# A two-layer hybrid attention block: stick-breaking heads taken in pairs, side work given out by a budget, three products laid ahead in the second mixer

## The chip, the cores and the metric

The kernel runs on one core of a Trainium2 chip. The metric is the device time of one execution in microseconds. Before the change three runs gave 1328.83, 1330.05 and 1330.17 us.

## The reference, cut to what matters

Two layers work on `x` (512 tokens, width 1024, float32). Each layer is a mixer and a gated feed-forward, and both end in `x = layer_norm(ALPHA * x + (1 + g) * y)`. Shifts, scales and gates are six rows of 1024 a layer: `silu(c) @ w_mod + b_mod`.

The mixer of layer 0 ("even") projects `h` once and runs two kinds of attention side by side, eight heads of 64 columns each:

```python
# stick-breaking, a head h; past = key before query
z = q @ k.T / 8
log_keep = where(past, log_sigmoid(-z), 0)
suffix = reverse_cumsum(log_keep) - log_keep
w = where(past, exp(log_sigmoid(z) + suffix), 0)
o = w @ v
# indexed ("dsa"): a score of 4 index heads picks the 128 best keys of a query
score = sum_h relu(q_idx[h] @ k_idx.T / 8) * w_idx[h]
o = softmax(q @ k[top_k(score)].T / 8) @ v[top_k(score)]
```

The mixer of layer 1 ("odd") is differential attention: `softmax(q1 k1) - lam * softmax(q2 k2)`, then an RMS norm of each head. Both mixers end in a product with `w_out`. All is held to float32 accuracy: a large product is made as three products of rounded parts (high x high, low x high, high x low).

## The kernel before, in words

Tokens stand in four blocks of 128. TensorE (PE) makes all products; a weight is split by `split_w` (L291) into a high half by ScalarE (ACT) and a low half `wl = raw - wh` by an engine of the list `low`, which is VectorE (DVE) except in mixer 2. One step of a dense product (`dense`, L349) is three products of 512 columns; eight steps make one tile of 128 output columns. The next tile's split is asked for at the fourth step.

The program is written as generators. `weave(main, fill, ratio)` (L255) runs an attention generator and, for each cost that it yields, lets the fill generator issue as much dense work, by its own yielded costs. `beside(main, side, every)` (L271) gives a side generator a step on every so many steps. The numbers yielded are prices in us that the code assumes. The framework then plans each engine's own queue ahead of time: an instruction that is earlier in the program goes first, unless its inputs or its buffer are not there yet in the plan, in which case a later one that is ready may take its place. At run time each queue is strictly in order.

The parts that the change touches:

- `sb_heads` (L821) is the stick-breaking attention. A head's scores are held transposed in three PSUM banks (`za`, `zb`, `zc`), as four strips of keys (`STRIP`, L818: 512, 384, 256 and 128 columns of queries). `scores_of(h)` makes the four strips, each with a bias product, then by spans abs, exp, ln on ACT, a max-add on DVE, the rounded copy `hi` on DVE (L840) and `lo = l - hi` on GpSimd (POOL, L841). `suffix(h)` adds the sums of later keys by 20 products of `hi` and `lo` with constant matrices and takes exp to `w`. `mix(hp)` multiplies the weights of two heads with `v`. Even heads lie in rows 0 to 63 of `q` and `k`, odd heads in rows 64 to 127.
- `index_scores` and `top_keys` (L760, L784) make the index scores and pick keys in 48 steps on DVE. `mod_side` (L187) makes one row of shifts or gates: 16 products of DVE (`macc`, L211) and a reduction on PE. In layer 0 three such rows (`mods_even`, L996) run beside mixer 1; `topk` and they are handed out with `beside`, one `topk` step to each dense step, one mod step to every fourth and to each step of the heads.
- `dsa_heads` (L920) is the indexed attention, a pipeline of units of 128 queries and two heads. `one` makes scores, masks them, takes exp and normalises `e` on DVE (L952); `two`, two units later, transposes `e`; `three` multiplies with `v`. Its fill is `even_fill` (L1008): the rest of the projections, then the first half of the product with `w_out` (`down_beside`) with a mod step on every second step.
- `rope` (L454) turns a projected tile: ACT copies it to `rq`, DMAs on SyncE's queue swap halves into `rt`, DVE and POOL multiply, DVE adds.
- `down_last` (L613) ends a mixer: eight outputs of four terms each, of which `lead` outputs have three terms laid ahead (`down_lead`), behind the last transposes. `LEAD1` is 2 for mixer 1, `LEAD2` 5 for mixer 2. As a token block's two outputs are there, it is normed (DVE and POOL) and transposed for the next stage.
- `last_norm` (L1198) is the end of the kernel. For the last block two thirds are finished on DVE and 256 columns on POOL (L1212, L1213), each with its own transfer.

## Time and profile before

| | us |
|---|---|
| median of three runs | 1330.05 |
| profiled execution, its own time | 1333.3 |
| its span | 1331.5 |
| PE busy (share of the span) | 1285.6 (97%) |
| DVE busy | 877.8 (66%) |
| ACT busy | 498.0 (37%) |
| POOL busy | 250.7 (19%) |
| mean granted clock of PE | 0.985 |

The profile is one execution. Busy times of PE hold the time that a product is under way, so neighbours overlap; how long a run of products takes is read from the distance of their starts. The arrow behind an idle time names what ended it. One product in float32 makes two records of PE here, one in the rounded type makes one.

### The profile page before, as it was taken

The page shows a single profiled execution, that of the slowest core. Times are in us where ns is not written, and L with a number is a line of the kernel's source. Part 1 is how long each engine was busy: PE and PEld are TensorE (multiplying, and loading weights), DVE is VectorE, ACT ScalarE, POOL GpSimd, SP SyncE. Part 2 cuts the span into 40 slices and gives each one's busy share as a digit, 9 for nine tenths or more (in the row PEclk, how much of TensorE's full clock was granted, in tenths as well). Part 3 has the DMA queues.
Part 4 walks back from the last instruction along what each step waited for, and adds up shares of the span by engine and source line. Part 5 has one row for each costly group of instructions (what it writes and reads, how often), then busy time and mean ns, then how long its engine had stood idle before and what let it go on. Part 6 is the DMA issues. An engine that isn't in the chain of part 4 may idle for free.

```text
span 1331.5 us, 17598 instructions
## 1 busy us (share of the span) xinstructions
PE 1285.6 (97%) x6707; PEld 1020.7 (77%) x6707; DVE 877.8 (66%) x1596; ACT 498.0 (37%) x888; POOL 250.7 (19%) x177
## 2 busy tenths in 40 slices
PE   6999998999999999999999999898899999999997
PEld 4767676668888888888888866676798888888885
DVE  3789996988866665665694377688766435335357
ACT  2445554554532222222244355564543321222221
POOL 0113223001800000000017244442170000000034
PEclk9999989899999999999999999899899999999999
DMA  9952234333265555555423422215225222223221
GB/s 259 284 175 95 84 114 137 103 119 103 83 219 160 191 173 173 184 178 184 147 67 112 127 64 82 86 56 173 75 86 175 95 95 95 95 95 108 99 79 63
DMA packets 134532, 169.47 MB, mean 127 GB/s; under 512 B 7816, under 2 KB 89392, under 8 KB 134448
## 3 DMA queue, kind: packets, MB, share of 16 engines
q1 hardware_dynamic: 133712, 167.34, 39.2%
q8 instruction: 52, 0.85, 0.3%
q10 hardware_dynamic: 576, 0.98, 0.2%
q14 instruction: 32, 0.26, 0.1%
q0 software_dynamic: 160, 0.03, 0.0%
HBM read 159.95 MB, written 2.10 MB: 122 GB/s over the span
## 4 chain that ended last, share of the span: by engine, by line
PE 77%; DVE 11%; DMA 3%; ACT 3%; issue 2%; POOL 1%; SPq 1%; POOLq 0%; ACTq 0%; DVEq 0%
PE po L320 13%; PE po L321 13%; PE po L322 13%; PE pd L320 7%; PE pd L322 7%; PE pd L321 7%; PE pf L321 2%; PE pf L322 2%; PE pf L320 2%; DMA wm<-in_w_mod_dram 2%; PE pv L320 1%; PE pv L321 1%; PE pv L322 1%; DMA rt<-rq 1%; PE zq L893 1%
## 5 line engine op out<-in xcount | busy, mean ns | idle before, releaser
L294 ACT ACTIVATE wh<-raw 128x1024 fp32r<-128x1024 f32 x174 | 183.9, 1065 | 523.3 <-PE po L321 291.7
L320 PE MATMUL po<-hh,wh 128*128 128x512 f32 x848 | 340.9, 402 | 0.0
L321 PE MATMUL po<-hl,wh 128*128 128x512 f32 x848 | 333.4, 393 | 0.0
L322 PE MATMUL po<-hh,wl 128*128 128x512 f32 x848 | 333.4, 393 | 0.0
L298 DVE TENSOR_TENSOR wl<-raw,wh 128x1024 fp32r<-128x1024 f32 x169 | 228.5, 1356 | 157.1 <-ACT wh L294 156.6
L320 PEld LDWEIGHTS po<-hh,wh 128*128 128x128 f32 x848 | 160.8, 190 | 38.3 <-issue 6.4
L322 PEld LDWEIGHTS po<-hh,wl 128*128 128x128 f32 x848 | 161.0, 190 | 34.4
L321 PEld LDWEIGHTS po<-hl,wh 128*128 128x128 f32 x848 | 161.1, 190 | 30.4
L321 PE MATMUL pd<-wl,hid_h 128*128 128x512 f32 x352 | 137.1, 389 | 0.0
L322 PE MATMUL pd<-wh,hid_l 128*128 128x512 f32 x352 | 137.0, 389 | 0.0
L320 PE MATMUL pd<-wh,hid_h 128*128 128x512 f32 x352 | 137.0, 390 | 0.0
L211 DVE SCALAR_TENSOR_TENSOR macc<-wm,silu_c,macc 128x512 f32<-128x512 f32 x140 | 109.8, 787 | 7.0 <-DMA wm<-in_w_mod_dram 4.7
L636 DVE TENSOR_TENSOR sg<-sg,po 128x512 f32<-128x512 f32 x40 | 27.5, 687 | 125.3 <-PE po L322 125.3
L504 POOL TENSOR_TENSOR lnv<-lnv,mhalf 128x1 f32<-128x1 f32 x16 | 11.7, 731 | 396.8 <-DVE lnv L502 396.8
L320 PEld LDWEIGHTS pd<-wh,hid_h 128*128 128x128 f32 x352 | 66.1, 188 | 14.0 <-issue 0.4
L321 PEld LDWEIGHTS pd<-wl,hid_h 128*128 128x128 f32 x352 | 66.1, 188 | 13.7
L322 PEld LDWEIGHTS pd<-wh,hid_l 128*128 128x128 f32 x352 | 66.1, 188 | 13.6
L481 DVE TENSOR_TENSOR yt<-pd,grow 128x512 f32<-128x512 f32 x88 | 58.5, 681 | 10.7 <-PE pd L322 10.5
L600 POOL TENSOR_TENSOR raw<-raw,grow 128x1024 f32<-128x1024 f32 x4 | 10.4, 2610 | 284.0 <-DMA raw<-in_w_down_dram 283.6
L320 PE MATMUL pd<-wh,o_h 128*128 128x512 f32 x128 | 57.7, 451 | 1.8 <-DVE yt L481 1.8
L321 PE MATMUL pd<-wl,o_h 128*128 128x512 f32 x128 | 52.0, 406 | 0.3 <-DVE wl L298 0.3
L322 PE MATMUL pd<-wh,o_l 128*128 128x512 f32 x128 | 52.1, 407 | 0.0
(280 smaller groups left out, 2057.0 us busy)
## 6 DMA issues: line engine op xcount, KB each, us to landing
wm<-in_w_mod_dram SPq DMA_DIRECT2D x56, 512.0 KB, 4.9
raw<-in_w_gate_dram SPq DMA_DIRECT2D x22, 1024.0 KB, 5.2
raw<-in_w_up_dram SPq DMA_DIRECT2D x22, 1024.0 KB, 5.2
wm<-in_w_mod_dram SPq DMA_DIRECT2D x80, 256.0 KB, 4.0
raw<-in_w_down_dram SPq DMA_DIRECT2D x16, 1024.0 KB, 5.0
raw<-in_w_in_odd_dram SPq DMA_DIRECT2D x12, 1024.0 KB, 5.3
raw<-in_w_in_even_dram SPq DMA_DIRECT2D x6, 1024.0 KB, 7.6
raw<-in_w_down_dram SPq DMA_DIRECT2D x12, 512.0 KB, 3.3
```

Source lines behind the costliest of these rows:

```text
L211: dve.scalar_tensor_tensor(a, t[:, k, :], silu_c[:, k0 + k:k0 + k + 1], a, op0=OP.mult, op1=OP.add)
L294: act.activation(oh, src, AF.Copy)
L298: e.tensor_tensor(ol, src, oh, op=OP.subtract)
L320: pe.matmul(o, lhsT=ah, rhs=bh, start=start, stop=False, skip_group_check=True)
L321: pe.matmul(o, lhsT=ah, rhs=bl, start=False, stop=False, skip_group_check=True)
L322: pe.matmul(o, lhsT=al, rhs=bh, start=False, stop=stop, skip_group_check=True)
L481: dve.tensor_tensor(t, o, grow[:, cs], op=OP.mult)
L504: norm_done["pow"] = pool.tensor_tensor(y, v[:, 1:2], mhalf[:, 0:1], op=OP.pow).ins
L600: pool.tensor_tensor(tt, tt, gate[:, HALF[h]].unsqueeze(1).to_broadcast([P, 2, S]), op=OP.mult)
L636: dve.tensor_tensor(g, g, o, op=OP.mult)
L893: pe.matmul(z, lhsT=q[a][own, cs], rhs=k[b][own, :n], start=(g == 0), stop=(g == 2), skip_group_check=True)
```

## The change

1. The stick-breaking scores are made for both heads of a pair, strip by strip: all score products of a set of strips, then all bias products. The set is either banks `zb` and `zc` ("late") or `za` ("first"). The order of a pair is suffix late, suffix first, mix, then the next pair's late and first scores; the output's copy in `mix` thus stands ahead of the next late scores. `hi` is copied by ACT, one strip behind the strip that ACT works on (`cast`). The weights of the second head lie in other buffers (`weights_of`). The yielded prices are those of `SB_COST`.
2. `topk` and the mods of layer 0 are one generator, `sums`: a mod step after every three `topk` steps. `give(time)` advances it by a budget in us; the heads give at fixed places and `paced` gives 0.65 of each fill step. `beside` hands a mod step to every step of `down_beside`.
3. While the heads run, the low halves of weights are made by POOL (`low_on(pool)`).
4. In `dsa_heads` POOL normalises `e` in place of DVE.
5. In `rope` POOL writes its product to the target and DVE adds to it in place.
6. `LEAD2` is 3 in place of 5.
7. In `last_norm` DVE finishes the last 256 columns too.
8. `mod_side` yields once more ahead of each reduction in the narrow form; `top_keys` yields its price.

The diff, cut to its core; of the functions inside `sb_heads` the old lines are those printed above, so the new ones stand alone.

```diff
+SIDE = 0.65
+SB_COST = (6.2, 3.0, 2.8, 1.0)
...
-LEAD2 = 5
+LEAD2 = 3
@@ -210,8 +212,7 @@
                         else:
                             dve.scalar_tensor_tensor(a, t[:, k, :], silu_c[:, k0 + k:k0 + k + 1], a, op0=OP.mult, op1=OP.add)
                     yield
-            if wide:
-                yield
...
-            pool.tensor_tensor(q, q, cos_t, op=OP.mult)
-            dve.tensor_tensor(dst, q, t, op=OP.add)
+            pool.tensor_tensor(dst, q, cos_t, op=OP.mult)
+            dve.tensor_tensor(dst, dst, t, op=OP.add)
...
-                yield
+                yield 0.27 * (i + 1) + 0.28
...
@@ -819,64 +820,104 @@
     SPAN = ((0, 0, 512), (1, 512, 1024), (2, 1024, 1280))
     def sb_heads(qk):
+        Z, HL, W, todo = {}, {}, {}, []
+        def cast():
+            hi, lo, l = todo.pop(0)
+            act.activation(hi, l, AF.Copy)
+            pool.tensor_tensor(lo, l, hi, op=OP.subtract)
+        def scores_of(hp, banks):
+            q, k = qk[hp]
             need(q, k)
+            for i in banks:
+                for j in range(2):
+                    Z[hp, i, j] = bank("z" + "abc"[i])
+            strips = [(s, *STRIP[s]) for s in (1, 3, 2, 0) if STRIP[s][0] in banks]
+            for s, i, f, _, n in strips:
+                for j in range(2):
+                    own = slice(64 * j, 64 * j + 64)
+                    pe.matmul(Z[hp, i, j][:, f:f + n], lhsT=k[own, P * s:P * s + P], rhs=q[own, P * s:S],
+                              start=(f == 0), stop=False, skip_group_check=True)
+            for s, i, f, _, n in strips:
+                for j in range(2):
+                    pe.matmul(Z[hp, i, j][:, f:f + P], lhsT=ident_r, rhs=bias_sb_r, start=False, stop=True, skip_group_check=True)
+            for j in range(2):
+                if (hp, j) not in HL:
+                    HL[hp, j] = ab("hi", F32R), ab("lo", F32R)
+                hi, lo = HL[hp, j]
+                for i, a, b in SPAN:
+                    if i in banks:
+                        zi, e, l = Z[hp, i, j][:, :b - a], slice(a, b), wd("l")[:, :b - a]
+                        act.activation(l, zi, AF.Abs)
+                        act.activation(l, l, AF.Exp, scale=-1.0)
+                        act.activation(l, l, AF.Ln, bias=1.0)
+                        dve.scalar_tensor_tensor(l, zi, 0.0, l, op0=OP.max, op1=OP.add)
+                        todo.append((hi[:, e], lo[:, e], l))
+                        if len(todo) > 1:
+                            cast()
+            if todo:
+                cast()
+        def weights_of(hp, j, a, b):
+            part = a >= S
+            if (hp, j, part) not in W:
+                if j == 0:
+                    w = ab("w")
+                    W[hp, j, 0], W[hp, j, 1] = w[:, :S], w[:, S:]
+                elif part:
+                    W[hp, j, part] = T("row", [P, D], F32, 2, "w")
+                else:
+                    W[hp, j, part] = r1("w")
+            return W[hp, j, part][:, a - S * part:b - S * part]
+        def suffix(hp, banks):
+            for j in range(2):
+                hl = HL[hp, j]
+                for s in (0, 1, 3, 2):
+                    i, f, _, n = STRIP[s]
+                    if i not in banks:
+                        continue
+                    for s2 in range(s, 4):
+                        _, _, c2, n2 = STRIP[s2]
+                        for op in hl:
+                            pe.matmul(Z[hp, i, j][:, f + n - n2:f + n], lhsT=negtri_r if s2 == s else negones_r,
+                                      rhs=op[:, c2:c2 + n2], start=False, stop=True, skip_group_check=True)
+                for i, a, b in SPAN:
+                    if i in banks:
+                        act.activation(weights_of(hp, j, a, b), Z[hp, i, j][:, :b - a], AF.Exp)
         def mix(hp):
+            o = Z[hp, 0, 1]
             for s, (_, _, c0, n) in enumerate(STRIP):
                 for j in range(2):
                     h = 2 * hp + j
+                    pe.matmul(o[64 * j:64 * j + 64, S - n:S], lhsT=v_sb[s][:, 64 * h:64 * h + 64], rhs=weights_of(hp, j, c0, c0 + n),
                               start=(s == 0), stop=(s == 3), skip_group_check=True)
             put_o(hp, o)
+        late, first = (1, 2), (0,)
+        scores_of(0, late)
+        scores_of(0, first)
+        yield SB_COST[0]
         for hp in range(4):
+            suffix(hp, late)
+            give(1.7)
+            yield SB_COST[1]
+            suffix(hp, first)
+            give(1.7)
+            yield SB_COST[2]
+            mix(hp)
             if hp < 3:
+                give(1.8)
+                scores_of(hp + 1, late)
+                give(1.8)
+                yield SB_COST[3]
+                scores_of(hp + 1, first)
+                give(1.2)
+                yield SB_COST[0]
     turned = [None]
...
             for j in range(2):
-                dve.tensor_scalar(es[j], es[j], rr[:, j:j + 1], None, op0=OP.mult)
+                pool.tensor_scalar(es[j], es[j], rr[:, j:j + 1], None, op0=OP.mult)
...
     topk = late(2, chain(index_scores(), top_keys()))
     drain(beside(proj_tokens(W, 1024, evac_v), topk, 1))
-    rest = beside(even_rest(), topk, 1)
     got_rows = []
 
...
     mods0 = mods_even()
-    rest = beside(rest, mods0, 4)
-    weave(beside(sb_heads(qk_sb), mods0, 1), rest, SB_FILL)
+    def sums():
+        for n, cost in enumerate(topk):
+            yield cost or 1.5
+            if n % 3 == 2:
+                next(mods0, None)
+                yield 0.85
+        for _ in range(4):
+            next(mods0, None)
+            yield 0.85
+    owed, side = [0.0], sums()
+    def give(time):
+        owed[0] += time
+        while owed[0] > 0:
+            got = next(side, None)
+            if got is None:
+                break
+            owed[0] -= got
+    def paced(main, rate):
+        for cost in main:
+            give(cost * rate)
+            yield cost
+    rest = paced(even_rest(), SIDE)
+    low_on(pool)
+    weave(sb_heads(qk_sb), rest, SB_FILL)
+    low_on(dve)
     for _ in topk:
         pass
...
             next(mods0)
-        yield from beside(down_beside(w_out_even[0], 0, oT[:4], rows[0, 2], True), mods0, 2)
+        yield from beside(down_beside(w_out_even[0], 0, oT[:4], rows[0, 2], True), mods0, 1)
         drain(mods0)
...
-        for e, q, cs in (((dve, sp, slice(0, 384)), (dve, act, slice(384, 768)), (pool, sp, slice(768, D))) if b == 3
-                         else ((dve, sp, HALF[0]),)):
+        for q, cs in ((sp, slice(0, 384)), (act, slice(384, 768)), (sp, slice(768, D))) if b == 3 else ((sp, HALF[0]),):
             t = xa[b][:, cs]
-            if e is dve:
-                dve.scalar_tensor_tensor(t, t, r, rows["b"][:, cs], op0=OP.mult, op1=OP.add)
-            else:
-                pool.tensor_scalar(t, t, r, None, op0=OP.mult)
-                pool.tensor_tensor(t, t, rows["b"][:, cs], op=OP.add)
+            dve.scalar_tensor_tensor(t, t, r, rows["b"][:, cs], op0=OP.mult, op1=OP.add)
             away(q, b, cs)
```

## Rows read from the trace of the kernel before

**Rows 1.** The page, part 1: busy us (share of the span) and instructions.

```profile
PE 1285.6 (97%) x6707; PEld 1020.7 (77%) x6707; DVE 877.8 (66%) x1596; ACT 498.0 (37%) x888; POOL 250.7 (19%) x177
```

**Rows 2.** Stretches of two stages: us, busy time of each engine, clock, DMA share.

```profile
95.90:228.70 132.80, 131.10 (x589) 90.83 (x588) 116.37 (x249) 71.29 (x138) 35.80 (x30) 0.95 0.35 110
228.70:301.90 73.20, 68.31 (x468) 46.82 (x468) 63.67 (x177) 38.62 (x100) 7.17 (x6) 0.95 0.34 112
```

**Rows 3.** PE in order of time, one head's scores: start us, us, what, count.

```profile
105.45 1.12 PE L830 MATMUL za<-q_sb,k_sb 64*128 64x512 f32 x2
106.51 0.33 PE L832 MATMUL za<-cst_r 128*128 128x128 f32 x1
106.76 0.91 PE L830 MATMUL zb<-q_sb,k_sb 64*128 64x384 f32 x2
...
109.33 0.44 PE L320 MATMUL po<-hh,wh 128*128 128x512 f32 x1
```

**Rows 4.** PE in order of time, two index heads one behind the other.

```profile
92.11 0.92 PE L777 MATMUL ix<-kix,qix 64*128 64x384 f32 x4
```

**Rows 5.** Stretches of lower granted clock (the column behind the busy times).

```profile
144.70:148.10 3.40, 3.40 (x9) 2.61 (x8) 3.40 (x9) 2.23 (x6) 0.66 (x1) 0.51 0.03 11
233.50:240.30 6.80, 6.59 (x30) 3.77 (x30) 5.33 (x18) 2.21 (x9) 0.59 (x1) 0.50 0.36 105
```

**Rows 6.** What PE waited for, whole span: us in total, times, longest.

```profile
PE zq L893 <- DVE kd_l L929: 4.3, 1, 4.3
PE po L1144 <- DVE on L1134: 4.0, 3, 2.6
```

**Rows 7.** Groups by line, 96 to 228 us: busy us, mean ns, idle before.

```profile
L841 POOL TENSOR_TENSOR lo<-l,hi 128x512 fp32r<-128x512 f32 (+1 forms) x24 | 27.5, 1151 | 84.4 <-DVE hi L840 58.2 <-PE ix L777 22.1 <-issue 4.1
L837 ACT ACTIVATE l<-l 128x512 f32<-128x512 f32 (+1 forms) x24 | 12.6, 560 | 0.3
L298 DVE TENSOR_TENSOR wl<-raw,wh 128x1024 fp32r<-128x1024 f32 x10 | 12.1, 1208 | 0.0
L294 ACT ACTIVATE wh<-raw 128x1024 fp32r<-128x1024 f32 x10 | 10.6, 1061 | 10.8 <-PE po L321 10.6
L840 DVE CAST hi<-l 128x512 fp32r<-128x512 f32 (+1 forms) x24 | 9.5, 407 | 0.0
L810 ACT ACTIVATE o_h<-ot 128x512 fp32r<-128x512 f32 x4 | 2.5, 632 | 0.1
```

**Rows 8.** Groups by line on POOL, whole span.

```profile
L298 POOL TENSOR_TENSOR wl<-raw,wh 128x1024 fp32r<-128x1024 f32 x5 | 12.4, 2480 | 7.0 <-ACT wh L294 3.7 <-issue 3.3
```

**Rows 9.** PE in order of time, end of mixer 2.

```profile
946.12 0.39 PE L321 MATMUL pd<-wl,o_h 128*128 128x512 f32 x1
946.34 0.39 PE L322 MATMUL pd<-wh,o_l 128*128 128x512 f32 x1
948.41 0.63 PE L523 MATMUL tx<-ct,xa 128*128 128x128 f32 x4 [1.69 <-DVE xa L509]
950.71 0.80 PE L320 MATMUL pd<-wh,o_h 128*128 128x512 f32 x1 [1.67 <-DVE yt L481]
```

**Rows 10.** Groups by line on DVE in the indexed stage.

```profile
L211 DVE SCALAR_TENSOR_TENSOR macc<-wm,silu_c,macc 128x512 f32<-128x512 f32 x9 | 6.9, 761 | 0.4 <-DMA wm<-in_w_mod_dram 0.4
```

**Rows 11.** One line's instructions: duration ns min/median/max, first and last start.

```profile
L952 DVE TENSOR_SCALAR e<-e,rr x32: 278/406/1411, 238.9 to 293.0; 128x128 f32<-128x128 f32 x8, 128x256 f32<-128x256 f32 x8, 128x384 f32<-128x384 f32 x8, 128x512 f32<-128x512 f32 x8
```

**Rows 12.** DVE in order of time, the last block.

```profile
1325.89 1.14 DVE L1210 SCALAR_TENSOR_TENSOR xa<-xa,lnv,lnb 128x384 f32<-128x384 f32 x2
```

**Rows 13.** POOL in order of time, the last block.

```profile
1326.15 1.60 POOL L1212 TENSOR_SCALAR xa<-xa,lnv 128x256 f32<-128x256 f32 x1 [0.43 <-DVE xa L1205]
1327.83 0.72 POOL L1213 TENSOR_TENSOR xa<-xa,lnb 128x256 f32<-128x256 f32 x1
```

**Rows 14.** DVE in order of time, beside POOL work.

```profile
991.88 3.41 DVE L298 TENSOR_TENSOR wl<-raw,wh 128x1024 fp32r<-128x1024 f32 x1
```

**Rows 15.** POOL in order of time, the same stretch.

```profile
991.36 6.19 POOL L543 TENSOR_TENSOR xa<-xa,lnb 128x1024 f32<-128x1024 f32 x2
```

46 lines of the change are left out of this document (1 added, 45 removed).

## The prediction

> **What bounds the kernel now.** I read the page's busy shares first, then the stretches, then single stretches of TensorE in order of time. TensorE (PE) is busy for 1285.6 of 1331.5 us [rows 1], so only two things can shorten the kernel: less time of PE per product, or less waiting in the few places where PE stands. The edits of any weight lie in two stages [rows 2]: stick-breaking attention from 95.9 to 228.7 us (132.8 us; PE 131.1 busy, DVE 116.4, ACT 71.3, POOL 35.8) and the indexed attention behind it (73.2 us; PE 68.3, DVE 63.7, POOL 7.2). So PE sets the pace of both, with DVE close behind it. The profiled execution took 1333.3 us, 1.8 outside the span and 3.25 above the median of 1330.05; I sum differences and take them from the median.
>
> **Scores by pairs (the main term).** In the old order one head's scores run alone: four products of 64 rows, each followed by a bias product of 128 rows, from 105.45 to the next fill product at 109.33, so 3.88 us a head and 7.76 a pair [rows 3]. A lone head's 384-column strip keeps PE 0.91 us (2 records). In the index scores, two heads that stand in different row halves are issued one behind the other: their two 384-column products take 0.92 us together (4 records) [rows 4]. So two row halves work at once, and the second head of a strip is nearly free. The new code issues the two heads of a strip one behind the other. For a pair I count: the 1280 columns of one head, 3.0 us in proportion to the 0.91 us of 384 columns, less the changes of shape that fall away as strips follow each other: I take 2.4; eight bias products in two runs of one shape, at under half of the 0.25 us that each keeps PE alone, from start to next start [rows 3]: 0.9 with their changes. That is 3.3 us, 4.45 less than 7.76, and 17.8 for four pairs. Bounds: if nothing overlapped, only changes of shape would go (some 0.6 us a head by the bias rows, 4.8 in all); if bias and changes cost nothing, 5.3 a pair, 21.
>
> **Clock.** In four stretches of 3.4 us of this stage the granted clock is about 0.5 (1.2 of 2.4 GHz), one is shown, and so it is in one of 6.8 us behind the wait at its end [rows 5]. Each 3.4 us at the lower level costs 1.7. The first of the four, at 100, follows a lone head's scores; the one at 233.5 follows PE's 4.3 us stand for kd_l [rows 6]. Paired scores leave fewer half-used stretches: I take two of four away, -3.4 us; bounds -10.2 (all, the seam's too) and +3.4 (two more).
>
> **New waits in the stage.** DVE loses the 24 casts (9.5 us) and the ten low halves of weights (12.1) and is no longer near its bound; ACT gains the 24 casts, about 24 x 0.56 = 13.4 us (0.63 each by the copy o_h, 0.56 with the narrow strips), and POOL ten subtractions of 2.48, 24.8 us [rows 7, 8]. ACT then has 85 and POOL 61 us of a stage of some 112: neither is a bound by its sum. As a chain it is tight: from late scores to their low halves ACT makes 4 strips x 3 passes x 0.56 + 4 casts x 0.56 = 9.0 us, then POOL 1.15 [rows 7], so about 10; PE has one fill step, the first strip's scores (1.2 by the same count) and ten steps between, at 0.68 a step (three products some 0.23 apart [rows 9]) 8.7 us. The second head's part is needed 1.4 us later, which about closes it. I take +1 us a pair, +4. Below, 0. Above, one weight split ahead of the strip on ACT (1.06) and one on POOL (2.48) at each of eight suffix calls: 28. Copying outputs ahead of the late scores only changes which of ACT's work comes first, and frees the bank that the first strip needs; 0.
>
> **Side sums.** The give() budget is 3.4 + 4.8 us a pair and 0.65 of each fill step; counting the yields, 44 of 49 top-key steps and 14 of 54 mod steps are out by the end of the weave, so five selection steps (0.82 us each by the code's own price, an order of size) and 26 more products of macc (0.76 [rows 10]) come into the indexed stage or into DVE's new slack ahead of it. No instruction is added, only order: the extra yield, SIDE and the changed beside() likewise. Against it stand the 32 normalisations that leave DVE (median 0.41 [rows 11], 13 us). DVE's 63.7 us of 73.2 become 63.7 - 13 + 20 + 4 = 75 if nothing is done ahead. But the stage before has over 30 us of DVE to spare, so I expect most to be done there. POOL needs for a 128x256 normalisation between 0.72 (its two-input neighbour) and 1.60 (the same operation, beside DVE work) [rows 12, 13]; in proportion to the columns (10,240 in all) 29 to 64 us for all 32. I take the lower end: the larger row runs beside a DVE operation for half of its time. A unit's transposes come two units later, some 9 us, which hides 2 x 1.3 of the widest; only the last unit shows. +1 us; bounds -4.3 (PE's stand for kd_l at the seam goes [rows 6]) and +29 (below). At the seam itself DVE stood for the landing of a rope transfer, which stays; 0.
>
> **Rope.** POOL writes its product to the target rather than in place; same instructions, one buffer free earlier. 0, bounds -1 and +1.
>
> **Three products laid ahead in mixer 2.** 18 products (4.1 us) move from before the last head's output to behind it. Before, PE ran out of work twice while the first blocks were normed: 1.69 us for xa L509 and 1.67 for yt L481, starts 948.41 and 950.71 [rows 9]. The first block can close up to 4.1 us sooner with 18 products still to come, so both stands (3.4 us) should be covered: -3.4. What is lost is cover ahead of the last head's output, where PE already stands 2.6 us for `on` [rows 6]; before that stand only some 19 of the 45 products were issued (counted in order of time), and 27 still suffice. Bounds -5.1 (a clock stretch with them) and +4.1 (all 18 missed).
>
> **The last quarter.** POOL's two operations end at 1328.55; DVE's second piece ends at 1327.03 and a third of 256 columns adds about 0.4 (two of 384 take 1.14) [rows 12, 13]: 1327.4, -1.1 us. Bounds -1.5 and 0 (if the transfer of the second piece ends last).
>
> **Sum.** -17.8 - 3.4 + 4 + 1 - 3.4 - 1.1 = -20.7; 1330.05 - 20.7 = 1309 us.
>
> **Rivals.**
> *The chain behind the scores takes half back.* If in each pair one split sits ahead of the strips on ACT and POOL (3.5 us), +14 in place of +4, and after each such stand a clock stretch (1.7) in place of the two removed: 1309 + 10 + 3.4 + 1.7 = 1324. For it: ACT's 9 us against PE's 8.7. Against: the order is planned, and PE waited hardly at all in this stage.
> *More goes than I count.* All four clock stretches and the seam's wait and stretch go too: 1309 - 3.4 - 4.3 - 3.4 = 1298. For it: DVE is freed. Against: the seam hung on a transfer.
> *POOL takes DVE's time (slower).* A DVE subtraction of 128x1024 that takes 1.21 as a rule [rows 7] took 3.41 beside POOL [rows 14, 15]. In the indexed stage 35 macc, five splits and eight xa sums of DVE have two inputs in SBUF; beside POOL the split loses 2.2, the others, half as wide, 1.1: 5 x 2.2 + 43 x 1.1 = 58 us if all are hit in full. At 1.60 us for 256 columns POOL is busy 64 us of 73; nearly each is hit then, but on average half way through, so 29 us fall on a DVE that is already full: 1309 - 1 + 29 = 1337. It is slower than before from about 22 us on: a POOL busy two thirds of the stage, with DVE's side work still in it. Against it: DVE's slack one stage ahead. The Trainium skill ("SBUF — State Buffer", two separate sides) states that rule: DVE operations with two SBUF inputs and GpSimd operations share one port pair, whoever starts first holds it for the whole instruction. The two rows of the split agree with it. Against it speaks the Trainium skill in "GPSIMD Engine Reference", engine selection: one-input work on GpSimd runs at about line rate, by which, as an estimate, a 256-column normalisation is near 0.2 us and the 32 take under 10; the row of 1.60 speaks against the page, and no row shows the operation undisturbed.
> *The pairs don't overlap.* The four-pass products come apart in the planned order or don't run at once: only the changes of shape are saved, 4.8 of 17.8, so 1322. The index rows speak against it.
>
> **Numbers.** Forecast (1301 to 1317) 0.60, half taken back 0.18, more 0.11, slower 0.07, no overlap 0.04. The range 1295 to 1324 leaves out the slower case and the far ends. A measurement of this kernel tells 0.2%, some 2.7 us, from no change: the first, the third and the last case are faster, of the second 0.14 (the rest of it 0.03 same and 0.01 slower): faster 0.89, same 0.03, slower 0.08.
>
> **What would show it.** Pair scores near 3.3 us with the two heads' starts some 10 ns apart; the stage near 113 us; hi on ACT, wl on POOL at about 2.5; no stand of PE at 948 to 951; the last transfer 1 us earlier. I am wrong if PE shows stands for `lo` or `wl` of several us in each pair, if the indexed stage grows beyond 80 us with DVE full, or if `e` on POOL holds the transposes.

## The result and the profile after

The changed kernel took 1339.65 us (median of 4 runs, 1336.95 to 1341.31), the kernel before 1329.65 beside it: a ratio of 1.0055 with a 95% interval of 1.0031 to 1.0079. It is slower by some 7 us by the ratio, where 21 less were forecast.

The page's first part, to set beside [rows 1]: TensorE is busy 16.7 us less, and the span (1339.4) is 7.9 longer. So its work went down, and waiting came in its place.

```profile
PE 1268.9 (95%) x6707; PEld 1011.1 (75%) x6707; DVE 867.0 (65%) x1531; ACT 506.3 (38%) x912; POOL 319.9 (24%) x217
```

The two stages of [rows 2], cut at the same places (0.5 us ahead of the first score, the first indexed score, 3.8 us behind the last indexed output). The columns are as there: length, busy time of each engine, clock, DMA share.

```profile
95.70:234.30 138.60, 116.23 (x579) 85.53 (x578) 100.12 (x203) 80.05 (x161) 56.24 (x39) 0.90 0.29 87
234.30:318.30 84.00, 75.84 (x505) 52.02 (x505) 63.24 (x163) 39.71 (x105) 43.21 (x35) 0.92 0.45 143
```

TensorE works 15 us less in the first stage, which is 5.8 longer; no other engine is full by its sum. The second is 10.8 longer with VectorE's work as before. In marks: from first score to last mix 125.6 us against 129.1, from there to the first indexed score (the seam) 12.4 against 3.1, indexed scores and outputs 80.2 against 69.4. Behind them the kernel gains: 3.8 in the differential stage, 5.3 at the end of mixer 2, 0.9 at the end.

One pair's scores in TensorE's order of time, to set beside one head's in [rows 3] (start, us, what, count of records):

```profile
96.22 1.03 PE L841 MATMUL zb<-q_sb,k_sb 64*128 64x384 f32 x8
97.09 0.60 PE L841 MATMUL zc<-q_sb,k_sb 64*128 64x256 f32 x4
97.62 0.66 PE L845 MATMUL zb<-cst_r 128*128 128x128 f32 x4
98.12 0.39 PE L845 MATMUL zc<-cst_r 128*128 128x128 f32 x2
98.43 1.13 PE L841 MATMUL za<-q_sb,k_sb 64*128 64x512 f32 x4
99.49 0.44 PE L845 MATMUL za<-cst_r 128*128 128x128 f32 x2
99.77 0.45 PE L321 MATMUL po<-hh,wh 128*128 128x512 f32 x1
```

A pair takes 3.55 us (96.22 to 99.77), against 7.76. The pairs overlap as forecast.

What TensorE waited for from 96 to 345 us, where [rows 6] has one wait of 4.3 in the same part of the kernel (in total, times, longest). `macc` is a modulation sum, `mh` and `ml` are its high and low half, which TensorE adds up; `hi` and `lo` are the halves of the stick-breaking sums:

```profile
PE pm L223 <- DVE ml L221: 6.5, 1, 6.5
PE pm L231 <- DVE macc L213: 3.8, 1, 3.8
PE ix L778 <- ACT w L890: 3.7, 1, 3.7
PE zb L886 <- POOL lo L829: 3.5, 6, 1.0
PE po L321 <- ACT q_sb L471: 3.4, 1, 3.4
PE pm L222 <- ACT mh L220: 2.9, 2, 2.4
```

And the waits behind these, of VectorE, of ScalarE (96 to 225) and of SyncE's load queue:

```profile
DVE macc L213 <- DMA wm<-in_w_mod_dram: 22.5, 15, 4.6
```

```profile
ACT hi L828 <- DVE l L856: 16.8, 8, 5.1
```

```profile
SPq L559 <- POOL wl L299: 44.5, 2, 28.4
```

The 2.4 us for `mh` and the 6.5 us for `ml`, at the seam, are not a wait for a sum: the last product of this sum began at 140.5. ScalarE made `mh` only at 224.80. VectorE made `ml` at 232.39, behind two products of the next sum that waited for their loads, a split and a mask step (ScalarE, then VectorE):

```profile
224.80 0.62 ACT L220 ACTIVATE mh<-macc 128x512 fp32r<-128x512 f32 x1
```

```profile
225.73 1.82 DVE L213 SCALAR_TENSOR_TENSOR macc<-wm,silu_c,macc 128x512 f32<-128x512 f32 x1 [1.40 <-DMA wm<-in_w_mod_dram]
230.39 0.75 DVE L213 SCALAR_TENSOR_TENSOR macc<-wm,silu_c,macc 128x512 f32<-128x512 f32 x1 [2.84 <-DMA wm<-in_w_mod_dram]
...
232.39 0.69 DVE L221 TENSOR_TENSOR ml<-macc,mh 128x512 fp32r<-128x512 f32 x1
```

The clock falls beside the stands. Two stretches, to set beside [rows 5]; the column behind the busy times is the granted clock, 0.50 is 1.2 GHz. The first begins 0.8 us behind three short stands (0.77, 0.91 and 0.31 us, for `hi` and `lo`), and the 3.7 us for `ix` lie in it. The second begins 1.1 us behind a stand of 2.4 us for `mh`, and the 6.5 us for `ml` lie in it:

```profile
110.60:124.30 13.70, 8.70 (x27) 6.47 (x27) 13.46 (x25) 8.06 (x16) 7.61 (x5) 0.50 0.43 131
226.60:243.70 17.10, 9.76 (x36) 5.94 (x36) 11.85 (x33) 5.81 (x18) 5.18 (x6) 0.50 0.46 154
```

Between the first score and the first feed-forward 44.4 us run at half clock, against 20.5 before.

The end of mixer 2: of the two stands in [rows 9] (1.69 and 1.67 us) one of 0.48 is left. And the last block on VectorE: its three pieces end at 1336.24, 4.7 us behind TensorE's last product; before, GpSimd ended 5.8 behind it [rows 13].

```profile
961.46 1.53 PE L524 MATMUL tx<-ct,xa 128*128 128x128 f32 x12 [0.48 <-DVE xa L510]
```

```profile
1334.71 1.53 DVE L1277 SCALAR_TENSOR_TENSOR xa<-xa,lnv,lnb 128x384 f32<-128x384 f32 x3
```

### The profile page after: what moved, and what is told of

Read it like the earlier page. It is cut to its first block, busy times and chain, and to the rows that moved or that the text cites. A ratio compares the mean times of both kernels' runs of the same rounds, so it can differ in the third digit from the quotient of the medians.

```text
span 1339.4 us, 17581 instructions
## 1 busy us (share of the span) xinstructions
PE 1268.9 (95%) x6707; PEld 1011.1 (75%) x6707; DVE 867.0 (65%) x1531; ACT 506.3 (38%) x912; POOL 319.9 (24%) x217
## 4 chain that ended last, share of the span: by engine, by line
PE 66%; DVE 15%; DMA 7%; ACT 5%; issue 4%; SPq 2%; POOL 1%; DVEq 0%; ACTq 0%; POOLq 0%
PE po L321 12%; PE po L322 12%; PE po L323 12%; PE pd L321 7%; PE pd L322 7%; PE pd L323 7%; DMA wm<-in_w_mod_dram 4%; DVE score L792 2%; DVE wl L299 2%; DVE macc L213 2%; DVE top L791 1%; DMA rt<-rq 1%; PE pv L321 1%; PE pv L322 1%; PE pv L323 1%
## 5 line engine op out<-in xcount | busy, mean ns | idle before, releaser
L299 DVE TENSOR_TENSOR wl<-raw,wh 128x1024 fp32r<-128x1024 f32 x159 | 224.6, 1416 | 173.9 <-ACT wh L295 173.6
L323 PEld LDWEIGHTS pd<-wh,hid_l 128*128 128x128 f32 x352 | 66.1, 188 | 13.7
L322 PEld LDWEIGHTS pd<-wl,hid_h 128*128 128x128 f32 x352 | 66.1, 188 | 13.7
```

The costliest lines, as they stand in the source:

```text
L299: e.tensor_tensor(ol, src, oh, op=OP.subtract)
L322: pe.matmul(o, lhsT=ah, rhs=bl, start=False, stop=False, skip_group_check=True)
L323: pe.matmul(o, lhsT=al, rhs=bh, start=False, stop=stop, skip_group_check=True)
```

## The experiments

Four edits, alone and together, put a part of the changed kernel back. They are named C, S, L and E here. Theories have letters of their own in the expectations, and the text always says "theory" with those:

```diff
# C: the cast on VectorE
-            act.activation(hi, l, AF.Copy)
+            dve.tensor_copy(hi, l)
# S: the side sums handed out as before
-    rest = paced(even_rest(), SIDE)
+    rest = beside(beside(even_rest(), topk, 1), mods0, 3)
-    weave(sb_heads(qk_sb), rest, SB_FILL)
+    weave(beside(sb_heads(qk_sb), mods0, 1), rest, SB_FILL)
-    owed, side = [0.0], sums()
+    owed, side = [0.0], iter(())
# L: the low halves of weights on VectorE
-    low_on(pool)
-    low_on(dve)
# E: the normalisation on VectorE
-                pool.tensor_scalar(es[j], es[j], rr[:, j:j + 1], None, op0=OP.mult)
+                dve.tensor_scalar(es[j], es[j], rr[:, j:j + 1], None, op0=OP.mult)
```

S is near the old order, not the same: the kernel before has a modulation step at every fourth fill step and more steps of the heads. By the last mix 38 of the 48 modulation products had run before, 21 in the changed kernel, 41 with S and 38 in the plain kernel.

**All runs in one table.** The stage is the time from the first score to the last mix; "stands" is TensorE's idle time in it, "half" its time at half clock, both added up over the profiled execution. "Own" is the stage less the stands and less half of the time at half clock: roughly what TensorE's products would take at full clock (roughly, since some stands lie in half-clock time). "Next" runs from the last mix to the last indexed output. The kernel before was timed beside each, and ratios are to be compared rather than medians; single profiles of one kernel differ by some us, so that a few us of one column alone prove nothing. Each edit also lets all queues be planned anew, so part of a small difference can be the new plan and not the part that was edited.

| kernel | us | ratio (95%) | stage | stands | half | own | next |
|---|---|---|---|---|---|---|---|
| before | 1329.65 | | 129.1 | 1.7 | 13.7 | 120.5 | 72.5 |
| changed | 1339.65 | 1.0055 (1.0031 to 1.0079) | 125.6 | 13.5 | 20.5 | 101.9 | 92.6 |
| C | 1342.1 | 1.0108 (1.0085 to 1.0131) | 128.2 | 16.1 | 23.9 | 100.2 | 92.3 |
| S | 1334.15 | 1.0032 (1.0009 to 1.0055) | 141.9 | 22.7 | 37.5 | 100.5 | 70.4 |
| L | 1337.35 | 1.0066 (1.0045 to 1.0087) | 124.7 | 13.5 | 20.5 | 101.0 | 91.8 |
| C S L | 1327.78 | 0.9985 (0.9967 to 1.0002) | 127.9 | 11.2 | 23.9 | 104.8 | 76.5 |
| C S L E, "plain" | 1321.62 | 0.9937 (0.9914 to 0.9960) | 127.9 | 12.7 | 20.5 | 105.0 | 70.7 |
| C S | 1334.19 | 1.0031 (1.0014 to 1.0047) | 136.8 | 18.3 | 30.7 | 103.2 | 73.6 |
| S L | 1327.73 | 0.9991 (0.9977 to 1.0004) | 133.8 | 18.4 | 27.3 | 101.8 | 71.8 |
| before, tail parts alone | 1325.66 | 0.9973 (0.9953 to 0.9993) | 127.0 | 0.1 | 13.7 | 120.1 | 73.6 |
| plain, one ScalarE pass | 1320.14 | 0.9927 (0.9897 to 0.9958) | 126.3 | 11.6 | 20.5 | 104.5 | 67.1 |
| before, one ScalarE pass | 1325.93 | 0.9983 (0.9954 to 1.0011) | 126.3 | 1.5 | 10.2 | 119.7 | 68.5 |
| C L E (sums new) | 1334.31 | 1.0026 (1.0005 to 1.0047) | 124.0 | 14.3 | 17.1 | 101.2 | 86.5 |
| plain, fill moved | 1326.36 | 0.9969 (0.9945 to 0.9993) | 129.6 | 13.6 | 20.5 | 105.8 | 72.8 |
| plain, half the keys | 1325.51 | 0.9959 (0.9936 to 0.9982) | 133.0 | 15.2 | 27.3 | 104.2 | 70.9 |
| before, half the keys | 1332.71 | 1.0005 (0.9979 to 1.0031) | 131.7 | 0.3 | 27.3 | 117.8 | 71.4 |
| S L E (cast on ScalarE) | 1322.66 | 0.9950 (0.9928 to 0.9973) | 135.8 | 18.6 | 27.3 | 103.6 | 65.6 |
| plain, mod steps later | 1327.69 | 0.9985 (0.9968 to 1.0002) | 127.8 | 15.3 | 20.5 | 102.3 | 71.8 |
| plain, max-adds first | 1326.29 | 0.9981 (0.9960 to 1.0003) | 135.1 | 16.3 | 27.3 | 105.2 | 67.2 |
| plain, both reliefs | 1314.71 | 0.9879 (0.9837 to 0.9921) | 123.9 | 11.8 | 17.1 | 103.6 | 66.9 |

**C: the cast on VectorE.**

> One line of the changed kernel is put back: the 24 casts hi run on VectorE behind their max-add, not on ScalarE. Theory A (ScalarE's queue stands for VectorE): in the changed kernel hi on ACT waits 16.8 us in 8 places for the max-add l, the longest 5.1, and TensorE stands behind it for ix (3.7) and q_sb (3.4), with half-clock stretches of 13.7 and 6.8 us after them. Then the waits of hi, ix and q_sb go, and the stick-breaking stage is shorter by 7.1 plus about half of 20.5 of clock, some 10 to 17 us: about 1325. Theory B (side sums come late): the cost lies at the seam and in the indexed stage, which this leaves as they are: the stage of the pairs gains at most 3, the time is 1336 to 1340, and zq still starts more than 9 us after the last mix.

It is slower: 1.0108, 7 us by the ratios, with intervals that lie apart. Theory A falls. Its row was right as a row, its reading was not: the cast stood 5.11 us because its input, the max-add, was late on VectorE, and on either engine it stands behind that. The stretch shows it (ScalarE, then VectorE, then GpSimd of the changed kernel):

```profile
99.79 0.94 ACT L855 ACTIVATE l<-l 128x512 f32<-128x512 f32 x2
...
106.88 0.63 ACT L828 ACTIVATE hi<-l 128x512 fp32r<-128x512 f32 x1 [5.11 <-DVE l L856]
```

```profile
98.70 2.20 DVE L213 SCALAR_TENSOR_TENSOR macc<-wm,silu_c,macc 128x512 f32<-128x512 f32 x1
...
106.17 0.67 DVE L856 SCALAR_TENSOR_TENSOR l<-zb,l 128x512 f32<-128x512 f32 x1
```

```profile
97.82 2.53 POOL L299 TENSOR_TENSOR wl<-raw,wh 128x1024 fp32r<-128x1024 f32 x1 [6.14 <-ACT wh L295]
```

ScalarE's last pass over this strip ends by 100.7; its max-add L856 begins at 106.17, behind index sums, top-key steps and modulation products of VectorE.

**S: the side sums as before.**

> The changed kernel, with only the handing out of the side sums as before: one top-key step at each fill step, one step of the modulation sums at each step of the heads and at every third fill step (42 of the 54 by count before the weave ends, against 14); no give(). Theory B: the macc products are spread over the stage of the pairs, their loads are done when the seam comes, so pm no longer stands for mh, ml and macc (2.4 + 6.5 + 3.8 us at 225 to 233 and 311), and the 17.1 us at half clock behind it go too: seam -9, indexed stage -8 to -11, time 1320 to 1324. Theory A: ScalarE's queue is the cause; the seam gains 3 at most, time 1334 to 1340, hi still waits some 16 us for l.

The seam and the indexed stage came back as theory B said (70.4 us against 92.6), but the stage of the pairs took 141.9: with the 18 modulation products that return to it (35 against 17) it is 16 us longer. The net gain by the ratio is 3 us, with intervals that overlap.

**L: the low halves of weights on VectorE.**

> The changed kernel, with the low halves of weights (wl) of the weave on VectorE again instead of GpSimd. Theory C (GpSimd's wl holds the raw buffer, and by it SyncE's load queue: SPq w_out stood 28.4 us for wl, and no load was issued before 186.6): the modulation loads start earlier, macc on VectorE is not empty from 150 to 190, the seam and the indexed stage lose 5 to 12 us; time 1328 to 1334. Theory B: the loads stand for their place in the order, not for GpSimd; the SPq wait moves to DVE wl or stays, the time is within 3 us of the changed kernel's 1340. The 12 us of splits on VectorE cost nothing or up to 4 in either.

No change against the changed kernel. While the sums are handed out late, who splits the weights does not matter; theory C falls as a cause by itself. SyncE's queue stands just as long, now for VectorE's split:

```profile
SPq L559 <- DVE wl L299: 33.3, 3, 28.4
```

**C, S and L together.**

> All three at once: casts and low halves on VectorE, side sums handed out as before; what stays of the change is the paired scores, the outputs ahead of the late scores, the normalisation on GpSimd, three products laid ahead, and the last quarter. If A and B together hold the cause, the stage of the pairs ends some 15 us earlier than before (scores -15.8 by their starts), the seam and the indexed stage are as before, and with -5.3 and -0.9 behind it the time is 1307 to 1313. If the stage stays within 5 us of before, VectorE, with 9.5 us of casts and 12 of splits again, is its bound, and the pairs can't be had without the moves: 1320 to 1326. If the indexed stage is still over 80 us, the normalisation on GpSimd is what holds it: 1318 or more.

0.9985: 9 us by the ratios below the changed kernel, though C and L alone won nothing. The stage is still no shorter than before, and the indexed stage alone takes 71.6.

**C, S, L and E: the plain paired kernel.** What is left of the change is the paired scores, the outputs ahead of the late scores, the rope's buffer, a modulation step at every step of `down_beside`, and the two tail parts.

> As the kernel with casts, low halves of weights and side sums put back (1327.8, ratio 0.9985), and now the 32 normalisations on VectorE too. There the transposes tp took 14.0 us from start to start in the indexed stage, against 10.0 before, 5.6 of them at half clock, and the seam's half clock was 20.5 us. Theory E (the normalisation on GpSimd delays the transposes, and the clock falls with it): tp back to 10 to 11 us, the indexed stage from 71.6 to 66 or 68, time 1322 to 1324. Theory F (TensorE just has too little work beside chains of other engines; whichever engine normalises): the stage stays at 70 to 73, time 1326 to 1329. If VectorE is full there, slower than 1329.

Theory E holds: 0.9937 against 0.9985, intervals apart, and this version is faster than both kernels. The indexed stage fell from 71.6 to 65.6 us, its half clock from 20.5 to 6.8: the normalisation's price is paid mostly in clock. One group of the normalisation on GpSimd, in the changed kernel:

```profile
L993 POOL TENSOR_SCALAR e<-e,rr 128x512 f32<-128x512 f32 x8 | 13.1, 1653 | 6.3 <-DVE rr L991 6.3
```

**C and S, then S and L.**

> Side sums as before and the casts on VectorE; the low halves of weights stay on GpSimd. With the side sums alone put back the stage of the pairs was 141.9 us (hi on ACT waited 21.2 us for l), with casts and low halves too 127.9. Theory A (the cast on ScalarE): 128 to 132 here, time 1326 to 1329, no wait of ScalarE for l. Theory C (the low halves on GpSimd, which take 2.4 us each and hold the raw buffers): 138 or more, time 1332 or more, with GpSimd's wl ahead of lo and the products po waiting for wl or q_sb.

> The counterpart: side sums as before and the low halves of weights on VectorE; the casts stay on ScalarE. Theory A: the stage of the pairs stays at 138 or more, hi waits over 15 us for l, time 1332 or more. Theory C: 128 to 132 us, time 1326 to 1329. If both this and its counterpart lie near 1330, the two shares add.

C S equals S (1.0031 and 1.0032), S L equals C S L (0.9991 and 0.9985): with the sums as before, the low halves on GpSimd cost 6 us, in the stage 8 to 9, and the engine of the cast nothing in time. In the profiles it only moves the wait: with the cast on VectorE the stage is 5 to 6 us shorter and what follows 3 to 5 longer. So theory C holds here, and theory A fell a second time. Three ways lead from a GpSimd split to TensorE (the split itself lasts 2.4 us for 1.2, `lo` queues behind it, VectorE's two-input operations are held, as the 2.20 us macc above beside the split of 97.82, which takes 0.75 alone); the runs don't part them.

**The tail parts alone, on the kernel before.**

```diff
-LEAD2 = 5
+LEAD2 = 3
# and the last quarter on VectorE, as in the change
```

> The kernel before with only two parts of the change: three products laid ahead in mixer 2 in place of five, and the last quarter on VectorE alone. The changed kernel won 5.3 us between the last transposes of the differential stage and the second feed-forward, and 0.9 at the end, while the profile of the stages before was its own. If these are the two parts' own gain, 1322 to 1325, a ratio of 0.995 to 0.997. If part of the 5.3 belongs to the clock's low stretches of before (933 and 950), which move with anything ahead of them, 1325 to 1328.

0.9973, 3.6 us: the forecast's 3.4 and 1.1 for these two. The plain kernel is 4.8 us below it by the ratios, but the intervals overlap: that is all that is left of the pairs' 16 us, and it is not clear of the noise.

**One of ScalarE's passes, with and without pairs.** Exp and Ln over the scores are left out, and of three passes Abs alone stays.

```diff
-                        act.activation(l, l, AF.Exp, scale=-1.0)
-                        act.activation(l, l, AF.Ln, bias=1.0)
```

> The plain paired kernel (casts, low halves, side sums and normalisations put back: 1321.6), with two of ScalarE's three passes over the scores left out (Exp and Ln; only Abs stays, so the weights are others). This shortens the way from the late scores to their suffix products by about 4 strips x 2 x 0.56 = 4.5 us and takes no work from TensorE. In the plain kernel the 160 suffix products take 33.9 us from start to start against 22.6 before, TensorE stands 12.7 us in the stage, and 20.5 us run at half clock. Theory G (with all six banks in one pair, nothing hides the chain from scores to suffix): suffix products 23 to 26 us, stands under 4, the stage 112 to 117 us against 127.9, time 1306 to 1312. Theory H (the suffix products are slow for another reason, such as their order or shapes): suffix products 31 or more, the stage 124 or more, time 1318 or more.

> The kernel before with the same two passes of ScalarE left out (its weights are others too). Theory G: there two heads alternate in three banks each, the chain of one lies under the suffix products of the other, and TensorE is the bound: no change, the stage 127 to 130 us, time 1326 to 1331. If ScalarE's chain bounded the kernel before as well, the stage would lose 8 us or more, time under 1322.

Before, no change that can be told: ScalarE did not bound it. With pairs the suffix products came down from 33.9 to 26.3 us, near theory G's 23 to 26, and the stage did not follow (126.3): in place of the stands at the suffix came one for the low half of a modulation sum, whose last product had begun at 99.4 and whose `ml` VectorE made at 137.76.

```profile
PE pm L223 <- DVE ml L221: 9.5, 1, 9.5
```

**The new sums alone.** C, L and E, without S.

> The plain paired kernel (1321.6), with the side sums handed out as in the changed kernel (give(), one modulation step at every third top-key step, the rest behind). Theory B (handed out late, the modulation sums wait for their loads in TensorE's queue at the seam and in the indexed stage): from zq back to the last mix 9 to 12 us in place of 5.0, the indexed stage 76 us or more in place of 65.6, time 1329 to 1335. Theory I (they cost only because GpSimd's wl held the raw buffers and its normalisations slowed VectorE): within 4 us of the plain kernel, 1320 to 1326.

1.0026 against 0.9937: handing the side sums out by the budget costs some 12 us by itself, where GpSimd has none of the work that the change moved to it. Theory B holds (the seam took 13.0 us; the indexed stage, with 73.5, less than its 76), theory I falls. Two of its waits of TensorE, the second again for the low half of a sum that was long done (last product 149.4, `ml` 229.87):

```profile
PE po L321 <- ACT q_sb L471: 10.5, 1, 10.5
PE pm L223 <- DVE ml L221: 6.6, 1, 6.6
```

**Fill moved ahead of the late suffix.**

```diff
-SB_COST = (6.2, 3.0, 2.8, 1.0)
+SB_COST = (8.2, 2.0, 1.8, 1.0)
```

> The plain paired kernel (1321.6) with the fill of each pair moved, not added: 8.2 in place of 6.2 between the scores and the late suffix, 2.0 and 1.8 in place of 3.0 and 2.8 behind the two suffixes (3 fill steps, some 2 us, move). Theory G: the stands at the late suffix (5.5 and some 3 us, each followed by 10 us of half clock) shrink, the stage loses 3 to 8 us, time 1314 to 1319. Rival: the stand only moves to the first suffix and to mix, where 2 us of cover are now lost four times: 1320 to 1325.

0.9969, no better than plain: the largest stand is now at the second pair's suffix (6.0 us), and 3.5 us stay at the third's.

**Half of the top-key steps, with and without pairs.**

```diff
-                dve.max(out=top, in_=sc)
-                dve.match_replace(out=sc, in_to_replace=top, in_values=sc, imm_value=TAKEN)
+                if r % 2 == 0:
+                    dve.max(out=top, in_=sc)
+                    dve.match_replace(out=sc, in_to_replace=top, in_values=sc, imm_value=TAKEN)
```

> The plain paired kernel (1321.6) with every second of the 48 top-key steps left out (its masks are others): some 26 us of VectorE's work less, at an even pace, nothing less for TensorE or ScalarE. Theory J (with the pairs VectorE, busy 9.4 to 10 of every 10 us from 95 to 195, is the bound; what TensorE saves it stands for VectorE): stands of TensorE in the stage from 12.7 us to under 3, half clock from 20.5 to under 8, the stage 112 to 117 us against 127.9, time 1305 to 1311. Theory G (the chain from scores over ScalarE to the suffix): the stage stays at 123 or more, time 1317 or more.

> The kernel before with the same steps left out (its masks are others too). Theory J: before, TensorE was the bound and VectorE just behind it, so only the clock's stretches can go: 1 to 4 us less, 1325 to 1329. If half the top-key steps won 8 us or more here too, VectorE was a bound before as well, and the pairs are not what brought it up.

Theory J falls: VectorE had 24 us less to do and the stage was 133.0. A stretch of this run shows why its sum is not the matter. VectorE stands idle for loads, and the max-add L857, whose input ScalarE had ready at 198.85, begins at 206.04 behind four steps that were put ahead of it:

```profile
201.82 0.75 DVE L213 SCALAR_TENSOR_TENSOR macc<-wm,silu_c,macc 128x512 f32<-128x512 f32 x1 [1.90 <-DMA wm<-in_w_mod_dram]
203.16 0.69 DVE L463 TENSOR_TENSOR rt<-rt,sin_t 128x512 f32<-128x512 f32 x1 [0.59 <-DMA rt<-rq]
203.96 0.69 DVE L465 TENSOR_TENSOR q_dsa<-q_dsa,rt 128x512 f32<-128x512 f32 x1
205.38 0.75 DVE L213 SCALAR_TENSOR_TENSOR macc<-wm,silu_c,macc 128x512 f32<-128x512 f32 x1 [0.73 <-DMA wm<-in_w_mod_dram]
206.04 0.69 DVE L857 SCALAR_TENSOR_TENSOR l<-zb,l 128x512 f32<-128x512 f32 x1
```

**The cast on ScalarE beside the rest of plain, and the modulation steps later.**

> The plain paired kernel with the 24 casts on ScalarE again, as in the changed kernel. Theory J: VectorE loses 9.5 us of its work in the packed part, the stage loses 3 to 8 us, time 1313 to 1319. Theory A (ScalarE's queue stands for VectorE's max-add): what VectorE gains ScalarE's queue loses, hi waits 15 us for l, time 1320 to 1325, as with the same step beside the normalisations on GpSimd, where the cast's engine made no difference.

```diff
-    rest = beside(beside(even_rest(), topk, 1), mods0, 3)
-    weave(beside(sb_heads(qk_sb), mods0, 1), rest, SB_FILL)
+    later = late(10, mods0)
+    rest = beside(beside(even_rest(), topk, 1), later, 2)
+    weave(sb_heads(qk_sb), rest, SB_FILL)
```

> The plain paired kernel with 12 of the 42 modulation steps moved out of the packed part: they begin at the 20th fill step and come at every second one (30 of 54 are out at the weave's end, against 14 in the changed kernel). Theory J: VectorE has some 3.5 of every 10 us to spare from 195 on, so up to 9 us of its work leave the packed part and the stage loses 3 to 6, time 1315 to 1319. Theory B: what is handed out late waits for its loads at the seam and in the indexed stage, so they lose as much or more, 1321 to 1327.

0.9950 and 0.9985. In the first theory A's numbers came in (ScalarE waited 16.9 us for max-adds): what VectorE gains, ScalarE's queue loses, and the cast's engine makes no difference a third time. Against S L (0.9991) this run has E alone, and the normalisation's price comes out again, 5.5 us with intervals apart. Moving 12 steps back costs 6 us by the ratios, at the edge of theory B's range, but not at its place: the first score begins at 99.8 us in place of 94.6, while the stage (127.8) is as in plain and what follows it 1.1 us longer. The loss lies in the order of work ahead of the stage, so this run speaks neither for theory B nor for J.

**Max-adds first.** The plain kernel's third pair has the same pattern as the stretch above. ScalarE's Ln is ready at 167.45; VectorE's order of time, then TensorE's:

```profile
168.77 1.21 DVE L299 TENSOR_TENSOR wl<-raw,wh 128x1024 fp32r<-128x1024 f32 x1
...
174.31 0.68 DVE L856 SCALAR_TENSOR_TENSOR l<-zb,l 128x512 f32<-128x512 f32 x1
```

```profile
176.04 0.69 PE L886 MATMUL zb<-hi,cst_r 128*128 128x384 f32 x1 [5.49 <-DVE hi L828]
```

and the clock from there on:

```profile
174.00:184.20 10.20, 7.30 (x24) 6.11 (x25) 10.20 (x28) 4.83 (x9) 6.53 (x6) 0.50 0.01 5
```

Over its 24 max-adds the time from the input to the start is 70.1 us (28.8 before). The edit ties side steps behind them:

```diff
+                        if hp:
+                            ahead_of.append(m.ins)
...
+    def tied(g):
...
+            with tc.issue_after(ahead_of.pop(0)) if ahead_of else nullcontext():
...
+    rest = beside(beside(even_rest(), tied(topk), 1), tied(mods0), 3)
# m: the max-add of a strip; the heads' own steps, tied(mods0), are left out here
```

> The plain paired kernel (1321.6), with an order written out on VectorE and nothing else: from the second pair on, each top-key or modulation step handed out behind a pair's scores is issued behind one of that pair's six max-adds, so they can't stand ahead of them in the queue. Theory K (VectorE's in-order queue: the max-add stands up to 7 us behind side steps): the stands at the suffix of the third pair (6.3 us, with 10 us of half clock behind it) go, those of the second shrink; the stage 118 to 123 us against 127.9, time 1311 to 1318. Theory G' (the chain is too long whichever order VectorE takes): the max-adds come on time, but the stands stay above 9 us in all, time 1320 to 1324. If the side steps held back make the seam and the masks late, a stand of TensorE for nm, kd_l or mh above 5 us shows there, time 1324 or more.

The lateness fell to 25.9 us, and to at most 0.6 us in the second and third pair. The stands did not fall (16.3 us), and the kernel is 5.9 us slower than plain by the ratios (0.9981). TensorE now stands for what was put behind:

```profile
PE pm L222 <- ACT mh L220: 4.7, 2, 3.7
PE pm L231 <- DVE macc L213: 4.7, 1, 4.7
PE zb L888 <- DVE hi L828: 2.8, 1, 2.8
```

So theory K had the place of single stands, and its forecast failed: at the third pair's suffix 3.7 us stay (2.8 and 0.9) with the order put right. Nor does the lateness order the kernels: it is 44.8 us in the changed one, and 121.2 in the fastest of all (both reliefs, next), where ScalarE is ready earlier.

**Both reliefs.** Of ScalarE's three passes one is left, and of four top-key steps one.

> The plain paired kernel (1321.6) with both reliefs at once: two of ScalarE's three passes over the scores and three of four top-key steps left out (weights and masks are others); TensorE's products are the same. Theory L (the stage is held by ScalarE and VectorE behind the scores together; each relief alone only passed the stand to the other's work): stands of TensorE under 4 us, half clock under 10, the stage 110 to 117 us against 127.9, time 1303 to 1311. Theory H' (TensorE's own order or shapes take the saving, whoever waits for whom): the stage 122 or more with stands under 6, time 1315 or more. If stands above 9 us remain at modulation sums, it is their loads, which neither relief touches.

0.9879, 7.7 us below plain by the ratios, with intervals that overlap: theory L's direction, not its size. The stands at the suffixes are 3.3 us in all; one stand of 8 us remains, with 10.2 us of half clock around it, for `ml`. The sum was done (its last product began at 97.8), and `mh` is made at 124.35; `ml` stands in VectorE's queue behind products of the next sum, which wait for their loads (VectorE, then TensorE):

```profile
126.87 0.75 DVE L213 SCALAR_TENSOR_TENSOR macc<-wm,silu_c,macc 128x512 f32<-128x512 f32 x1 [2.50 <-DMA wm<-in_w_mod_dram]
...
130.45 0.75 DVE L213 SCALAR_TENSOR_TENSOR macc<-wm,silu_c,macc 128x512 f32<-128x512 f32 x1 [1.69 <-DMA wm<-in_w_mod_dram]
...
135.25 0.68 DVE L221 TENSOR_TENSOR ml<-macc,mh 128x512 fp32r<-128x512 f32 x1
```

```profile
135.99 0.80 PE L223 MATMUL pm<-ml,cst_r 128*128 128x512 f32 x1 [8.03 <-DVE ml L221]
```

Taking off that one stand and half of its stretch would leave 111 us for the stage, inside theory L's 110 to 117; that is a subtraction, and no run shows it.

## Why the prediction was wrong

- **Scores by pairs** (-17.8): right in mechanism and nearly in size. From start to start scores and bias products take 15.1 us in the stage against 31.0, and mix 2.1 less, which was not forecast. "Own" in the table is 100 to 106 us in every paired kernel and 118 to 121 in the four without pairs.
- **New waits in the stage** (+4) and **Clock** (-3.4): the first step that failed. Stands went from 1.7 to 13.5 us and half clock from 13.7 to 20.5, worth 11.8 and 3.4: +15 where the two steps had +0.6. The rival "The chain behind the scores takes half back" had this price nearly (14 and the clock), but another place: it put it at a split ahead of the strips on ScalarE and GpSimd. The rows have single stands at VectorE's queue, where the max-add stands behind side steps, and then wherever else a side product of TensorE's queue hangs on VectorE; but with the max-adds on time the stands stayed, so this is where they were seen and not shown as their cause. Each relief that was tried moved the stands, and 11 to 23 us of them stayed in all sixteen paired kernels.
- **Side sums** ("no instruction is added, only order", +1 with the normalisation): the second step that failed, and the dearest: some 12 us. It argued that VectorE's slack in the stage of the pairs would draw the sums forward. The slack was there (92.7 us busy of the 126), and 21 of the 48 products had run by the last mix, against 38 before. A modulation product needs its load, loads are asked for one ahead on SyncE's in-order queue, and that stood up to 28.4 us for a raw buffer. GpSimd's split is not the cause: the queue stood as long for VectorE's in the run L. At the seam it was not products that were missing but the reduction of a sum done over 80 us earlier, whose `ml` stood behind the next sum's products; why ScalarE's `mh` came so late is not shown. In the four pairs of kernels that differ in S alone the new order costs 3 us (changed and S, intervals overlap), 10 (C and C S), 10 (L and S L) and 12 (C L E and plain).
- **The normalisation on GpSimd** (in the same +1): 6 us, by the run with E (5.5 in the second pair of runs). Its 32 instructions take 39.5 us, inside the 29 to 64 of the working; that a unit's transposes "come two units later" did not hide them.
- **The low halves on GpSimd**, which stood only as a bound of the new waits: 6 us with the sums as before, nothing with the new sums. So a split on GpSimd, where the rival of the chain had put its price, is a part of it. The parts don't add: 12, 6 and 6 are more than the 16 us between the changed and the plain kernel.
- **The rival "POOL takes DVE's time"** came nearest in time (1337) for another reason. VectorE's macc lasted 0.95 us on average from 95 to 320 us against 0.90 before, 2 us for 39 of them, not 29. Single ones were held as it said (2.20 for 0.75); the Trainium skill ("SBUF — State Buffer", two separate sides) states that, and the trace agrees.
- **Three products laid ahead** (-3.4) and **the last quarter** (-1.1): right; 5.3 and 0.9 in the changed kernel's trace, 3.6 together as runs of their own. **Seam** (0): 9.3 us, as part of the side sums. **Rope** (0): nothing seen, and it was not run alone. **The cast on ScalarE** (in the new waits) gained 7 us in the changed kernel and nothing with the sums as before.

Shown by runs: the prices of the side sums, of the low halves and of the normalisation; that the cast's engine has none with the sums as before; that before, neither ScalarE's passes nor the top keys bounded the stage. Only argued: why pairs make TensorE stand where single heads did not. Before, two heads of three banks each took turns, and one head's suffix lay over the other's chain; a pair holds all six banks, so its chain has only ten fill steps beside it. Pairs with more banks were not tried. Open, too, is how the kernels would do with the modulation loads asked for earlier, or with a sum's `mh` and `ml` ahead of the next sum's products: the stand for such an `ml` took 6.5 to 9.5 us in five of the paired kernels, and no run moved it alone.

## What to carry to other kernels

When a second engine is nearly as busy as the one that sets the pace, time taken from the first may not be gained: ask, for each product that becomes early, which side step stands ahead of its input, and expect that putting one such order right moves the stand, as it did here. A stand of TensorE can cost more than itself, as the clock goes down with it (a stand of 5.5 us, and 10.2 us at half clock that begin inside it). Side work that is only handed out later takes its loads and reductions along: count the queue that carries the loads, and look where the last small step of a finished sum stands in its queue.

## What had not been expected of the hardware

A normalisation with one input in SBUF took GpSimd 0.60, 0.92, 1.24 and 1.56 us at the least for 128, 256, 384 and 512 columns, VectorE 0.28, 0.34, 0.41 and 0.48 in the plain kernel: some three times as long for the wide ones (the profile's spans on GpSimd are rough). The Trainium skill ("GPSIMD Engine Reference", engine selection) has one-input work there at roughly line rate; the measurement decides, and it speaks against it.
